# PSUM banks of the state space part: 3, 4 and 1 in place of 2, 5 and 1

## The chip, the cores and the metric

The kernel runs on one core of a Trainium2 chip. The metric is device time in microseconds (us) of one launch. A core has a matrix engine (TensorE, PE in the rows), three engines for elementwise work (VectorE or DVE, ScalarE or ACT, GpSimd or POOL), a queue engine (SyncE, SP) and DMA engines. TensorE writes its results to PSUM, which has eight banks of 128 x 512 floats; the other engines read them there.

## The reference

An encoder trunk of two layers works on x (256 tokens x 1024) and on a memory of 256 tokens. Layer 0 mixes tokens by a bidirectional diagonal state space layer (S5) with a gated output, layer 1 by dilated attention; each layer then attends to the memory and has an MLP of width 4096. What matters here is the state space layer, and the keys and values of the memory:

```
def s5_direction(u, lam_re, lam_im, log_dt, b_re, b_im, c_re, c_im, reverse):
    ...
    bu_re = jnp.einsum('bsgc,gpc->bsgp', u, bbar_re)
    bu_im = jnp.einsum('bsgc,gpc->bsgp', u, bbar_im)
    ...
    _, _, xr, xi = lax.associative_scan(combine, (a_re, a_im, bu_re, bu_im),
                                        reverse=reverse, axis=1)
    return jnp.einsum('bsgp,gcp->bsgc', xr, c_re) - jnp.einsum('bsgp,gcp->bsgc', xi, c_im)

def memory_cross_attention(h, mem_n, w_q, w_kv, w_o, g_q, g_k):
    ...
    kv = (mem_n @ w_kv).reshape(bsz, mlen, 2, MEM_HEADS, MEM_HEAD_DIM)
```

There are 64 groups of 16 channels, 64 states each, and two directions. The keys and values are a product of 256 x 1024 by 1024 x 2048 for each of the two layers.

## The kernel before

The program is written as straight code, and a scheduler decides in what order the instructions stand on each engine and which free PSUM bank a tile gets. Tiles of PSUM come from three pools: `psa()` for accumulators (pool pa), `psb()` for everything of the chunks (pb) and `pss()` (ps). The sizes of the pools are the three numbers of `banks`. A tile that finds no free bank waits for the last reader of the tile that had it.

The state space layer goes over eight chunks of eight groups, numbered 0 to 7. For each chunk there are these steps:

- **Weighing-in** (`s5_weigh_in`): VectorE forms V in six operations (L1053, L1054, L1055, twice), TensorE transposes it into two `psb` tiles (L1060, four transposes each), ScalarE copies them to VT (L1062). V and VT have one buffer each.
- **Drive**: TensorE multiplies VT with the input into two `psb` tiles (L1099, 32 instructions).
- **Scan**: VectorE turns the drive (L1114 to L1119), scans it (L1123, twice) and turns it back (L1126 to L1131), in place in the two banks of the drive; the last two write xt. ScalarE prepares R for the scan (L1109, L1110) and copies xt to its place behind it (L1134, L1135).
- **Impulse**: TensorE multiplies the weights of the chunk (L1162, 16 instructions, one `psb` tile), ScalarE copies the result (L1167), VectorE adds to it (L1169, twice), ScalarE's queue writes it to memory (L1172) and reads it back in another layout as M (L1178, four issues).
- **Read**: TensorE multiplies the scan's states and M (L1191, L1194; 24 instructions, one `psb` tile), ScalarE applies the gelu (L1197, tile G), TensorE transposes G (L1203, another `psb` tile), ScalarE rounds it (L1207) and VectorE takes the rest (L1208).

GpSimd prepares the turns of each scan and the weights of each read meanwhile.

Between the steps of the chunks stand the memory products: three of the four halves of the keys and values (`memory_part` through `gemm32`). They have six blocks of 512 columns; a block has two `psa` tiles and 16 matmul instructions (L248, fp32, 128 x 512), 96 instructions in all. The trace has two records for each fp32 matmul instruction. ScalarE evacuates the tiles (L334). Behind the state space part the banks are split 4 and 4. There the last quarter of the memory product runs (L207 to L209, in three passes of rounded parts, whose weights ScalarE rounds at L161 and VectorE at L162), then the gated output and everything else.

Of the kernel before, what the change touches and what calls it, by code (L numbers as in the profile page):

```python
# [1269 lines left out]
def trunk(tc, a, stages=("s0", "x0", "m0", "d1", "x1", "m1")):  # L1270
    with ExitStack() as ctx:
        k = Trunk(ctx, tc, a)
# [21 lines left out]
        keys = [None, None]  # L1294
        if "s0" in seq:
            kvt = tc.alloc_tile_pool(name="kvt", bufs=1)
            with k.banks(2, 5, 1):
                with tc.tile_pool(name="s5", bufs=1) as ph:
                    with tc.tile_pool(name="s5p", bufs=1) as pr:
                        k.load_gains(pr, early, nc.sync)  # L1300
                        k.s5_load(pr, kv[0][1], kv[1])
                        k.s5_params(pr)
                        mT = [k.memory_in(0, kvt, kv[0][1])]
                        k.s5_norm(ph, kv[0][0].rearrange("p a b -> p (a b)"))
                        k.s5_tables(ph)
                        k.s5_b(ph)
                        turns = k.s5_turns(pr, ph, k.h.rearrange("p t c -> p (t c)"))
                        k.s5_weigh_in(ph, 0)
                        k.s5_c(ph, pr)
                        k.s5_skip(ph, pr)  # L1310
                        k.s5_input(ph)
                        mr = k.row_rstd(kv[0][1], "mem")
                        mT.append(k.memory_in(1, kvt, kv[0][1]))
                    gT = k.new_x()
                    with tc.tile_pool(name="s5m", bufs=1) as mp:
                        k.s5(mp, ph, turns, gT)
                        k.load_gains(mp, late, nc.sync)
                        k.bias_rows()
                xin()
                k1 = right("k1")  # L1320
                k.wq = right("wq")
                k0 = tc.alloc_tile_pool(name="k0", bufs=1, side="right")
                k.memory_part(0, 0, kv[0][0], mT[:1], mr, k.kvw)
                k.memory_part(0, 1, kv[0][1], mT[:1], mr)
                k.memory_part(1, 0, kv[1][0], mT[1:], mr)
        else:
            with k.banks(4, 4), tc.tile_pool(name="kvt", bufs=1) as kvt:
                k.load_gains(kvt, early, nc.sync)
                k.load_gains(kvt, late, nc.sync)
                k.bias_rows()  # L1330
                mem = kvt.tile([P, 2, D], F32, tag="mem", name="mem")
                k.memory_load(mem)
                mr = k.row_rstd(mem, "mem")
                k1 = right("k1")
                k.wq = right("wq")
                k0 = tc.alloc_tile_pool(name="k0", bufs=1, side="right")
                for q in range(2):
                    if "x%d" % q in seq:
                        mT = [k.memory_in(q, kvt, mem)]
                        for i in range(2):  # L1340
                            k.memory_part(q, i, kv[q][i], mT, mr)
                        keys[q] = k.key_parts(q, k.key_norms(q, kv[q][0], kvt), (k0, k1)[q])
                xin()
# [69 lines left out]
```

## Time and profile before

| | us |
|---|---|
| runs | 1066.17, 1064.74, 1066.33 |
| median | 1066.17 |
| profiled execution | 1063.59 |
| its span in the trace | 1061.8 |

The span is the time between the first and the last instruction of the profiled execution; the metric lies 1.8 us above it. The state space part takes about the first 208 us of it. In the rows "PEclk", the number behind the busy times of a window, is the share of TensorE's full clock that was granted.

### The profile page before, as it was taken

What the parts mean: (1) busy time and instruction counts of PE and PEld (TensorE: products, weight loads), DVE (VectorE), ACT (ScalarE), POOL (GpSimd) and SP (SyncE); (2) the same over time, 40 slices, a digit from 0 to 9 for tenths busy, and PEclk for the clock granted to TensorE, in tenths of its full rate; (3) what the DMA queues carried; (4) which work ended last, traced back from release to release, by engine and by line L of the source; (5) the groups of instructions that cost most, each with busy time, mean ns of one, the idle gap of its engine ahead of it and who ended that gap; (6) DMA issues with size and microseconds to landing.
All of it is one profiled execution on the core that took longest, in us unless ns stands there. A gap on an engine that the chain in (4) does not pass through costs nothing.

```text
span 1061.8 us, 17001 instructions
## 1 busy us (share of the span) xinstructions
PE 1012.3 (95%) x6591; PEld 830.8 (78%) x6591; DVE 696.8 (66%) x1108; ACT 576.5 (54%) x1030; POOL 210.7 (20%) x186
## 2 busy tenths in 40 slices
PE   4888889989999999999999999999999999999998
PEld 3454555568898998899878878878788989889996
DVE  7798995456586645544587777778747775544444
ACT  7453553576675644444555656667545655444443
POOL 3998981030000011000040030000200001100000
PEclk8898899999999999999999999999999999999999
DMA  9322233465543455565565555555415244555552
GB/s 199 104 90 70 56 108 112 129 218 182 179 136 109 166 192 191 170 192 192 180 213 165 159 168 178 159 162 149 149 60 173 106 157 162 178 193 185 188 188 100
DMA packets 98429, 163.80 MB, mean 154 GB/s; under 512 B 16704, under 2 KB 27116, under 8 KB 98092
## 3 DMA queue, kind: packets, MB, share of 16 engines
q1 hardware_dynamic: 89052, 158.84, 47.1%
q10 hardware_dynamic: 9296, 3.87, 1.4%
q8 instruction: 52, 0.85, 0.3%
q14 instruction: 29, 0.24, 0.1%
HBM read 160.70 MB, written 3.83 MB: 155 GB/s over the span
## 4 chain that ended last, share of the span: by engine, by line
PE 78%; DVE 12%; ACT 3%; issue 1%; POOL 1%; ACTq 0%; DVEq 0%
PE psa L208 14%; PE psa L209 14%; PE psa L207 14%; PE psb L279 6%; PE psb L283 6%; PE psb L281 6%; PE psa L405 4%; PE psa L248 3%; PE psb L390 2%; DVE wlo L162 2%; DVE V L1055 1%; PE psb L534 1%; DVE psb L1123 1%; ACT whi L161 1%; PE psb L673 1%
## 5 line engine op out<-in xcount | busy, mean ns | idle before, releaser
L162 DVE TENSOR_TENSOR wlo<-raw,whi 128x1024 fp32r<-128x1024 f32 x264 | 333.0, 1262 | 229.1 <-ACT whi L161 226.4
L161 ACT CAST whi<-raw 128x1024 fp32r<-128x1024 f32 x264 | 276.6, 1048 | 224.2 <-PE psa L209 139.2
L207 PE MATMUL psa<-whi,xs 128*128 128x512 f32 x448 | 177.8, 397 | 0.5 <-ACT sg L1238 0.5
L209 PE MATMUL psa<-whi,xs 128*128 128x512 f32 x448 | 176.8, 395 | 0.0
L208 PE MATMUL psa<-wlo,xs 128*128 128x512 f32 x448 | 176.3, 394 | 0.0
L279 PE MATMUL psb<-xs,whi 128*128 128x256 f32 x512 | 145.3, 284 | 0.0
L281 PE MATMUL psb<-xs,whi 128*128 128x256 f32 x512 | 145.3, 284 | 0.0
L283 PE MATMUL psb<-xs,wlo 128*128 128x256 f32 x512 | 145.1, 283 | 0.0
L292 POOL TENSOR_TENSOR sq<-rl 128x512 f32<-128x512 f32 x32 | 40.0, 1252 | 524.0 <-ACT rl L291 524.0
L209 PE MATMUL psa<-whi,hl 128*128 128x512 f32 x256 | 101.6, 397 | 0.0
L208 PE MATMUL psa<-wlo,hh 128*128 128x512 f32 x256 | 101.6, 397 | 0.0
L207 PE MATMUL psa<-whi,hh 128*128 128x512 f32 x256 | 101.5, 396 | 0.0
L248 PE MATMUL psa<-raw,mT 128*128 128x512 f32 x192 | 97.6, 654 | 2.9 <-ACT k L334 2.9
L279 PEld LDWEIGHTS psb<-xs,whi 128*128 128x128 f32 x512 | 98.3, 192 | 0.9 <-DVE xs L184 0.4
L281 PEld LDWEIGHTS psb<-xs,whi 128*128 128x128 f32 x512 | 98.3, 192 | 0.5
L283 PEld LDWEIGHTS psb<-xs,wlo 128*128 128x128 f32 x512 | 98.4, 192 | 0.0
L207 PEld LDWEIGHTS psa<-whi,xs 128*128 128x128 f32 x448 | 84.3, 188 | 16.9 <-ACT sg L1238 0.9
L209 PEld LDWEIGHTS psa<-whi,xs 128*128 128x128 f32 x448 | 84.2, 188 | 16.6
L208 PEld LDWEIGHTS psa<-wlo,xs 128*128 128x128 f32 x448 | 84.3, 188 | 15.9
L248 PEld LDWEIGHTS psa<-raw,mT 128*128 128x128 f32 x192 | 37.5, 207 | 43.2 <-issue 38.1
L209 PEld LDWEIGHTS psa<-whi,hl 128*128 128x128 f32 x256 | 48.3, 189 | 11.5
L207 PEld LDWEIGHTS psa<-whi,hh 128*128 128x128 f32 x256 | 48.3, 189 | 11.0
(330 smaller groups left out, 1542.0 us busy)
## 6 DMA issues: line engine op xcount, KB each, us to landing
raw<-in_mlp_w SPq DMA_DIRECT2D x128, 512.0 KB, 3.7
raw<-in_attn_w_qkv SPq DMA_DIRECT2D x72, 512.0 KB, 3.6
raw<-in_xattn_w_kv SPq DMA_DIRECT2D x32, 512.0 KB, 3.9
raw<-in_s_w_glu SPq DMA_DIRECT2D x16, 512.0 KB, 4.3
raw<-in_xattn_w_q SPq DMA_DIRECT2D x16, 512.0 KB, 3.4
raw<-in_xattn_w_o SPq DMA_DIRECT2D x16, 512.0 KB, 3.5
raw<-in_attn_w_o SPq DMA_DIRECT2D x8, 512.0 KB, 3.9
bias_d<-bias_o SPq DMA_DIRECT2D x1, 1536.0 KB, 8.8
```

The costliest lines, as they stand in the source:

```text
L161: self.nc.scalar.copy(hi, src)
L162: self.nc.vector.tensor_sub(lo, src, hi.bitcast(F32))
L207: nc.tensor.matmul(acc[t], xh[:, k0 + k, sl], hi[:, k % 2, :], start=st, stop=False)
L208: nc.tensor.matmul(acc[t], xh[:, k0 + k, sl], lo[:, k % 2, :], start=False, stop=False)
L209: nc.tensor.matmul(acc[t], xl[:, k0 + k, sl], hi[:, k % 2, :], start=False, stop=en)
L248: nc.tensor.matmul(acc[t], xT[:, k + q, t * P:(t + 1) * P], raw[:, q, :], start=k + q == 0, stop=k + q == KT - 1)
L279: nc.tensor.matmul(o, hi[:, k % 2, fs], xh[:, kt, :], start=st, stop=False, skip_group_check=True)
L281: nc.tensor.matmul(o, hi[:, k % 2, fs], xl[:, kt, :], start=False, stop=False, skip_group_check=True)
L283: nc.tensor.matmul(o, lo[:, k % 2, fs], xh[:, kt, :], start=False, stop=en, skip_group_check=True)
L292: nc.gpsimd.tensor_mul(sq, rl, rl)
L390: self.nc.tensor.matmul(out, x[p], w[q], start=start and i == 0, stop=stop and i == 2)
L405: nc.tensor.matmul(o, p[:, kt, ts], q[:, k, :], start=kt == 0 and t == 0 and i == 0, stop=kt == 7 and t == 1 and i == 2, skip_group_check= ...
```

## The change

The two numbers say how many banks the accumulators of the memory products get and how many the tiles of the chunks get. Two and five become three and four; the third pool keeps its one bank.

```
         if "s0" in seq:
             kvt = tc.alloc_tile_pool(name="kvt", bufs=1)
-            with k.banks(2, 5, 1):
+            with k.banks(3, 4, 1):
                 with tc.tile_pool(name="s5", bufs=1) as ph:
```

Everything else follows from the scheduler, which places the instructions anew. On TensorE, this is the difference between drive 0 and drive 2, early in the loop over the chunks. L1099 is a drive, L1162 an impulse, L1060 the transposes of a weighing-in, L248 a memory product.

```order
 L1099 MATMUL psb<-u_503,VT 64x64 x32
-L248 MATMUL psa<-raw,mT 128x512 x3
 L1060 MATMUL psb<-ident,V 128x128 x8
 L248 MATMUL psa<-raw,mT 128x512
 L1099 MATMUL psb<-u_503,VT 64x64 x32
+L248 MATMUL psa<-raw,mT 128x512 x6
 L1162 MATMUL psb<-wk,bb 32x112 x16
-L248 MATMUL psa<-raw,mT 128x512 x10
+L248 MATMUL psa<-raw,mT 128x512 x5
 L1060 MATMUL psb<-ident,V 128x128 x8
-L248 MATMUL psa<-raw,mT 128x512 x3
+L248 MATMUL psa<-raw,mT 128x512 x8
```

Products move behind drive 1: from three, one, ten and three, 17 in all, to one, six, five and eight, 20 in all. Further on in the loop about ten products stand between two drives in the change, and the eight transposes of a weighing-in are split four and four with products between. Counted over the program, 73 of the 96 products stand ahead of drive 7 before, and 86 in the change; 23 and 10 follow it.

On TensorE at the end of the state space part, from the products ahead of read 7 on (L1203 there is the transpose of chunk 6), the kernel before has these rows:

```order
L248 MATMUL psa<-raw,mT 128x512
L1203 MATMUL psb<-ident,G 64x64 x8
L248 MATMUL psa<-raw,mT 128x512 x11
L1191 MATMUL psb<-W,xs 64x64 x4
L1194 MATMUL psb<-M,u_503 64x64 x2
```

The changed kernel has these at the same place:

```order
L248 MATMUL psa<-raw,mT 128x512
L1203 MATMUL psb<-ident,G 64x64 x8
L248 MATMUL psa<-raw,mT 128x512
L1191 MATMUL psb<-W,xs 64x64 x4
L1194 MATMUL psb<-M,u_503 64x64 x2
```

Eleven products ahead of read 7 have become one. Of the four products that stand between read 7 and the first L207 before, none is left in the change.

On VectorE at the end of scan 7, L1208 of chunk 6 moves from between the operations of the scan to behind them, as this piece of the difference shows (the L162 of mp belongs to what follows the state space part).

```order
 L1126 TENSOR_TENSOR tmp<-psb,xs 128x512
 L1127 TENSOR_TENSOR tmp<-psb,xs 128x512
-L1208 TENSOR_TENSOR xs<-psb,xs 128x256
 L1128 TENSOR_TENSOR psb<-psb,xs 128x512
 L1129 TENSOR_TENSOR psb<-psb,xs 128x512
 L1130 TENSOR_TENSOR xt<-tmp,psb 128x512
 L1131 TENSOR_TENSOR xt<-tmp,psb 128x512
+L1208 TENSOR_TENSOR xs<-psb,xs 128x256
```

The scan's last operations no longer stand behind L1208. In the same way L1208 of chunk 0 moves from the start of scan 2 to behind it, and L1169 of chunk 0 from scan 0 to behind it, into the weighing-in that follows. Behind the state space part, 16 transposes of the keys (L379) move on TensorE behind the first products of the gated output.

## Rows read from the trace of the kernel before

**Rows 1.** The page: the span, and busy time of each engine.

```profile
span 1061.8 us, 17001 instructions
...
PE 1012.3 (95%) x6591; PEld 830.8 (78%) x6591; DVE 696.8 (66%) x1108; ACT 576.5 (54%) x1030; POOL 210.7 (20%) x186
```

**Rows 2.** Windows: length; busy PE, PEld, DVE, ACT, POOL (instructions); PEclk; DMA share; GB/s.

```profile
60.00:171.00 111.00, 94.51 (x1090) 56.16 (x1091) 103.39 (x153) 50.39 (x95) 92.90 (x78) 0.88 0.29 88
171.00:208.66 37.66, 36.71 (x345) 19.18 (x343) 15.90 (x24) 16.72 (x29) 0.00 (x0) 1.00 0.36 107
208.66:1061.00 852.34, 838.26 (x4866) 728.05 (x4866) 530.65 (x809) 472.47 (x832) 76.62 (x56) 1.00 0.52 167
```

**Rows 3.** VectorE's timeline in the loop: start, us, engine, line, operation, [idle <-releaser].

```profile
60.07 0.69 DVE L1114 TENSOR_TENSOR tmp<-psb,xs 128x512 f32<-128x512 f32 x1
...
69.19 0.23 DVE L1169 SCALAR_TENSOR_TENSOR kx<-eye,dc,psb 128x16 f32<-128x16 f32 x1 [1.80 <-ACT kx L1167]
...
97.31 0.42 DVE L1208 TENSOR_TENSOR xs<-psb,xs 128x256 fp32r<-128x256 f32 x1 [3.52 <-ACT xs L1207]
...
144.02 0.69 DVE L1114 TENSOR_TENSOR tmp<-psb,xs 128x512 f32<-128x512 f32 x1
...
154.18 0.68 DVE L1053 TENSOR_TENSOR tmp<-pss,bb 128x512 f32<-128x512 f32 x1
...
160.34 0.69 DVE L1114 TENSOR_TENSOR tmp<-psb,xs 128x512 f32<-128x512 f32 x1
```

**Rows 4.** TensorE's timeline in the loop: a product's wait, drive 5.

```profile
64.07 1.18 PE L248 MATMUL psa<-raw,mT 128*128 128x512 f32 x2 [2.93 <-ACT k L334]
...
138.94 1.16 PE L1099 MATMUL psb<-u,VT 64*64 64x64 f32 x64
```

**Rows 5.** Windows of L248 alone: length; busy PE, PEld (records); PEclk; DMA share; GB/s.

```profile
24.00:60.00 36.00, 21.97 (x36) 7.92 (x36) 0.86 0.36 90
60.00:171.00 111.00, 52.05 (x106) 20.64 (x107) 0.88 0.29 88
171.00:208.66 37.66, 23.59 (x52) 8.95 (x50) 1.00 0.36 107
```

**Rows 6.** TensorE's timeline in the tail, up to the first L207.

```profile
189.59 9.71 PE L248 MATMUL psa<-raw,mT 128*128 128x512 f32 x22
199.23 0.45 PE L1191 MATMUL psb<-W,xs 128*64 128x64 f32 x8
...
201.81 1.13 PE L248 MATMUL psa<-raw,mT 128*128 128x512 f32 x2
...
204.49 2.84 PE L248 MATMUL psa<-raw,mT 128*128 128x512 f32 x6
...
208.66 0.50 PE L207 MATMUL psa<-whi,mp 128*128 128x512 f32 x1 [0.95 <-ACT k L334]
```

**Rows 7.** TensorE's timeline at read 0.

```profile
87.00 0.70 PE L1191 MATMUL psb<-W,xs 128*64 128x64 f32 x8 [3.64 <-DVE xt L1130]
...
91.14 5.10 PE L248 MATMUL psa<-raw,mT 128*128 128x512 f32 x6
```

**Rows 8.** Window at read 0, columns as in rows 2.

```profile
88.00:92.00 4.00, 4.00 (x40) 2.89 (x38) 3.83 (x8) 3.91 (x7) 3.84 (x4) 0.50 0.00 0
```

**Rows 9.** VectorE's timeline at scan 7.

```profile
174.42 0.69 DVE L1114 TENSOR_TENSOR tmp<-psb,xs 128x512 f32<-128x512 f32 x1 [3.55 <-issue]
...
190.11 0.42 DVE L1208 TENSOR_TENSOR xs<-psb,xs 128x256 fp32r<-128x256 f32 x1 [0.60 <-ACT xs L1207]
...
192.25 0.68 DVE L1131 TENSOR_TENSOR xt<-tmp,psb 128x512 f32<-128x512 f32 x1
```

**Rows 10.** ScalarE's timeline in the tail (ACTq: its DMA issues).

```profile
190.17 2.53 ACTq L1178 DMA_DIRECT2D M<-kd  x4
192.96 1.04 ACT L1134 COPY xs<-xt 64x1024 f32<-64x1024 f32 x1 [2.88 <-DVE xt L1131]
...
201.98 0.38 ACT L1197 ACTIVATE G<-psb 128x256 f32<-128x256 f32 x1 [6.92 <-PE psb L1194]
```

More of the change, by code (lines that the diff above doesn't have):

```diff
@@ L1296, in trunk @@
             kvt = tc.alloc_tile_pool(name="kvt", bufs=1)
-            with k.banks(2, 5, 1):
+            with k.banks(3, 4, 1):
                 with tc.tile_pool(name="s5", bufs=1) as ph:
```

## The prediction

> **What bounds the kernel now.** I read the page first: a span of 1061.8 us, and TensorE busy for 1012.3 us of it [rows 1]. That average of 95% hides stages, so I cut the span into windows next [rows 2]. From 208.66 us on, TensorE works 838.26 of 852.34 us at a granted clock of 1.00; nothing in PSUM's split can shorten that. Between 60 and 171 us it is VectorE that is full (103.39 of 111 us) while TensorE has 94.51 us of work and a mean clock of 0.88. Between 171 and 208.66 us TensorE is full again (36.71 of 37.66) and VectorE is not (15.90). So the state space part is a loop on VectorE, which leaves TensorE room, and a tail on TensorE, which does what didn't fit. Work that moves from the tail into the loop is a gain as long as VectorE doesn't feel it.
>
> VectorE's timeline shows the loop's beat [rows 3]: scan 0 begins at 60.07, scan 6 at 160.34. Between two scans lies the weighing-in of a later chunk, six operations, 154.18 to 160.34, so 6.2 us. In the timeline there are two stalls: 1.80 us at L1169, which waits for the copy of the impulse response, and 3.52 us at L1208, which waits for L1207. TensorE's timeline shows what the memory products wait for a bank: once, 2.93 us [rows 4]. And by the windows of L248 the 192 records of the products (two for each of the 96 instructions) take 21.97 + 52.05 + 23.59 = 97.61 us [rows 5]; 0.883 us each would be 84.8 us (9.71 us for 22 records, 11 products [rows 6]). The other 12.8 us is the half clock: TensorE waited 3.64 us for scan 1, and from there on three products take 5.10 us, 1.70 us each [rows 7]; in 88 to 92 us the granted clock is 0.50, the lower level, 1.2 GHz [rows 8].
>
> **What the change does, and its cost.**
>
> *Thirteen products move forward.* By the order, 73 products stand ahead of drive 7 before, 86 in the change; 23 and 10 follow it. The third bank lets a product of the next block be issued before the last block is evacuated. In the tail 13 x 0.883 = 11.5 us of TensorE's work goes; in the loop it comes.
>
> *Is there room in the loop?* The loop's TensorE work would be 94.51 + 11.5 = 106.0 us, in 111 us less the two stalls, 105.7. That is full on paper, but 12.8 us of it is the half clock, paid wholly before 171 us (at 171 to 208.66 the clock is 1.00, and 52 records at 0.44 us are 23.0 of the 23.59). With TensorE fuller its wait of 3.64 us, behind which the clock fell, becomes shorter. Work other than products is 94.51 - 52.05 = 42.5 us there, 6.1 us for each of seven chunks; with ten products at full clock, 8.8 us, a chunk is 14.9 us. VectorE's beat at the end of the loop is 160.34 - 144.02 = 16.3 us [rows 3]. It fits, with 1.4 us to spare.
>
> *One bank less for the chunks.* Each drive needs two of four banks and now takes those of the scan before; the order shows that from drive 3 on it waits for the scan's last operation (L1131). In before that happens already at drives 5 to 7: drive 5 begins at 138.94 and VectorE goes into scan 5 at 144.02 without a stall [rows 3, 4], since the weighing-in of 6.2 us lies between; the drive takes 1.16 us. So the drive may come up to 6.2 - 1.16 = 5.0 us late at no price. I cost the bank at 0 in the loop. Without that cover each late microsecond is paid in each of the last five chunks. Behind a late drive on TensorE stand the impulse and read of the same chunk, and for these VectorE waits at L1169 and L1208.
>
> *The two stalls.* L1169 of chunk 0 goes behind the scan, into the weighing-in, and L1208 of chunk 0 behind scan 2: what they waited for is then done. So -1.80 and -3.52, -5.3 us for the loop. Bounds: 0 (L1208 of a later chunk stalls in its place) and -5.3; I take -5.3, since scan 5, with an L1169 and an L1208 inside it as the later scans of the change have them, takes 10.2 us from 144.02 to 154.18 and the timeline shows no wait in it [rows 3].
>
> *The tail.* Scan 7 starts behind a wait of 3.55 us for drive 7 [rows 9]. In the change half of the chunk's transposes wait for scan 6 to give a bank back; behind them stand three products (2.65 us) and the drive itself (1.16 us), in sum 3.8 us and a little: about the same, so nothing is gained there. Up to the scan proper the order is unchanged. L1208 of chunk 6 then leaves VectorE's row in scan 7: -0.60 for its wait and -0.42 for itself, -1.0 us [rows 9]. The last scan, which ended at 192.93, ends at 192.93 - 5.3 - 1.0 = 186.6 us.
>
> *Read of chunk 7.* In before it begins at 199.23, 6.30 us after the scan, for 11 products stand ahead of it (189.59 + 9.71 us [rows 6]). In the change one product does, so it waits for the two copies of 1.04 us on ScalarE. These stand behind four DMA issues, 2.53 us from 190.17 [rows 10], which move with the loop alone: 184.9 to 187.4. Then 2.1 us of copies: read at 189.5, against 199.23: -9.7 us.
>
> *What that empty TensorE costs.* Its last product now ends about 4 us before read 7. [rows 7] has the same figure: after a wait of 3.64 us, read 0 ran from 87.00 to 91.14, 4.14 us, at the lower clock; read 7 in before took 199.23 to 201.81, 2.58 us [rows 6]. So +1.6 us (bounds 0 and 1.6). Behind read 7 comes a hand-over on ScalarE: G at 201.98, then casts, to the first L207 at 208.66, 6.7 us [rows 6, 10]. Before, products (1.13 + 2.84 us) lay in it, so that the wait ahead of L207 was 0.95 us; now none do. The hand-over itself stays (its casts and copies are the same, except two L334 that were done earlier; I take 0 for these, they were partly hidden). But L207 would start at the lower clock. Bounds: 0, and a cold stretch as long as that of [rows 7], 87.00 to 96.17, 9.2 us for work of 2.58 + 2.65 us at full clock, so 4.0 us. I take the middle, 2.0.
>
> **Sum.** -9.7 + 1.6 + 2.0 = -6.1 us. Behind 208.66 us only 16 transposes of keys move; 0. The profiled execution took 1063.59 us, 1.8 us more than its span; it becomes 1057.5. The median of the runs is 1066.17, and 1066.17 - 6.1 = 1060.1 us. About 0.2%, 2.1 us, is what a measurement can tell here.
>
> **The rivals.**
>
> *Nothing comes of it (about 1066).* For it: the products waited only once for a bank, 2.93 us, so the third bank removes no wait worth the name; what moves is work, and if TensorE stays at the lower clock for the same 12.8 us in the loop, then 106.0 us doesn't fit there, the late drives eat the 5.3 us of stalls, and what read 7 gains over that (9.7 - 5.3 = 4.4 us) goes to the two cold starts (at their bounds 1.6 + 4.0 = 5.6). Sum: between -1.2 and +1.2. Against it: drive 5 is chained to the scan in before too, and ran in 1.16 us there [rows 4].
> The Trainium skill has a rule that speaks for this rival: its page "TensorE: Matmul & The Clock Gate", section "A second HAM failure mode: psum-queue depth-cycling", tells of a kernel that went round its PSUM banks and lost clock between bursts, so that throughput fell although a single product was as fast as elsewhere. By that rule going round three banks beside four would keep the lower clock in the loop, and the time would be this rival's. The trace agrees in so far as the clock falls in the loop, but it does so behind the wait for scan 1 [rows 7], and with two banks; no row here shows it to depend on their number.
>
> *Slower (about 1070).* The mechanism: the four banks chain each drive to the scan before, and the chunk to the drive. If a drive comes later than those 5.0 us, VectorE stalls, the scan ends later, the bank comes later, TensorE waits longer and goes to half clock: ten products then take 17.0 instead of 8.8 us, and a chunk costs 14.9 + 8.2 = 23.1 us and, with the rest of its work slow too, up to 25, where VectorE's beat is 16.3. From a stall of 6.1 / 5 = 1.2 us in each of the five chained chunks on, the gain is gone; one chunk at half clock, some 9 us, brings 1069 to 1070. Against it: the products in the loop are what keeps TensorE busy, and there are more of them.
>
> *More (about 1056.5).* No cold start, -9.7 us. For it: no row shows the clock behind an empty stretch at this place, and before it TensorE will have worked without a break. Against it: [rows 7] shows it fall behind a stretch of the same size.
>
> **How the numbers follow.** My forecast's family (a gain of 3 to 9.7 us, the last rival in it with 0.15) has 0.69, nothing 0.17, slower 0.14. The forecast's own range is 1056 to 1063. For 8 in 10 the range reaches into the middle rival on the upper side: from 1055 (the last rival, less the 1.4 us by which the runs of before differ among themselves) to 1067.
>
> **What would show it.** Right: scan 6 starts about 155 us instead of 160.34, no VectorE stall over 1 us between scans 0 and 6; no product between L1203 of chunk 6 and read 7 but one; read 7 at 189 to 190; L207 at about 200; the clock below 1 there for some microseconds. Wrong: stalls at L1114 (the drive late) or L1208 in chunks 3 to 6, a clock of 0.5 in the loop longer than before, a hand-over longer than 6.7 us, or a stretch behind it that takes longer than 852 us by more than 4.

## The result

The changed kernel takes 1056.46 us (four runs, 1055.19 to 1057.14); the kernel before took 1065.45 us in the four runs beside them (1064.40 to 1066.33). The ratio is 0.9918, with a 95% interval of 0.9906 to 0.9930, so 9.0 us less, between 7.5 and 10. Run again on the chip of the last experiments it gave 1056.37 against 1064.84 us, 0.9925 [0.9909, 0.9941]. The forecast was 1060.1 us in a range of 1055 to 1067.

The profiled execution of the changed kernel took 1056.39 us. Its page begins like this (compare [rows 1]):

```profile
span 1054.6 us, 17000 instructions
...
PE 1008.3 (96%) x6591; PEld 829.1 (79%) x6591; DVE 693.5 (66%) x1108; ACT 577.0 (55%) x1030; POOL 210.2 (20%) x186
```

TensorE's busy time fell by 4.0 us, the span by 7.2. These are the windows of the loop (scan 0 to scan 6), of the tail up to the first L207, and of the rest; columns as in [rows 2]:

```profile
62.58:153.62 91.04, 86.74 (x1036) 49.44 (x1036) 88.95 (x135) 48.95 (x94) 87.90 (x75) 1.00 0.32 96
153.62:199.84 46.22, 37.30 (x404) 20.38 (x402) 26.40 (x43) 20.68 (x37) 6.72 (x6) 0.90 0.35 109
199.84:1053.80 853.96, 840.66 (x4866) 730.58 (x4866) 530.78 (x810) 471.96 (x831) 76.62 (x56) 1.00 0.51 166
```

The loop of the kernel before, cut in the same way at its scans, was this:

```profile
60.07:160.34 100.27, 86.27 (x1024) 51.12 (x1024) 92.90 (x134) 47.12 (x87) 89.66 (x76) 0.88 0.30 90
```

The loop is 9.2 us shorter, and its granted clock is 1.00 where it was 0.88; TensorE does 86.74 us of work in it, where it did 86.27 in 9 us more before; it stands empty for 4.3 us of the loop, before for 14.0. The tail has a clock of 0.90 now, and TensorE stands empty for 9 us of it.

VectorE's timeline gives the points to hold against [rows 3] and [rows 9]:

```profile
62.58 0.69 DVE L1114 TENSOR_TENSOR tmp<-psb,xs 128x512 f32<-128x512 f32 x1 [0.66 <-PE psb L1099]
...
153.62 0.69 DVE L1114 TENSOR_TENSOR tmp<-psb,xs 128x512 f32<-128x512 f32 x1
...
165.32 0.37 DVE L1169 SCALAR_TENSOR_TENSOR kx<-eye,dc,psb 128x16 f32<-128x16 f32 x2 [1.27 <-ACT kx L1167]
167.93 0.69 DVE L1114 TENSOR_TENSOR tmp<-psb,xs 128x512 f32<-128x512 f32 x1 [2.23 <-issue]
...
184.84 0.68 DVE L1131 TENSOR_TENSOR xt<-tmp,psb 128x512 f32<-128x512 f32 x1
```

And TensorE's timeline the end of the tail, which answers to [rows 6]:

```profile
183.90 1.13 PE L248 MATMUL psa<-raw,mT 128*128 128x512 f32 x2
188.84 0.45 PE L1191 MATMUL psb<-W,xs 128*64 128x64 f32 x8 [3.81 <-issue]
...
197.98 0.69 PE L489 MATMUL psb<-junk,tb 33*24 33x160 f32 x2 [1.72 <-DMA junk<-in_bias_onehot]
199.84 0.79 PE L207 MATMUL psa<-whi,mp 128*128 128x512 f32 x1 [1.17 <-ACT junk L490]
```

The ledger of the two profiled executions, stretch by stretch:

| stretch | before | after | difference | forecast |
|---|---|---|---|---|
| up to scan 0 | 60.07 | 62.58 | +2.5 | 0 |
| scan 0 to scan 6 | 100.27 | 91.04 | -9.2 | -5.3 |
| scan 6 to the end of scan 7 | 32.59 | 31.90 | -0.7 | -1.0 |
| end of scan 7 to read 7 | 6.30 | 3.32 | -3.0 | -3.4 |
| read 7 to L207 | 9.43 | 11.00 | +1.6 | +1.6 |
| L207 to the end | 853.1 | 854.8 | +1.6 | +2.0 |
| sum | 1061.8 | 1054.6 | -7.2 | -6.1 |

Four of the six terms are where they were forecast, to within 0.4 us. The loop gave 3.9 us more, and the start took 2.5 us; neither was forecast. Between scans 6 and 7 VectorE waits 1.27 us for an impulse and 2.23 us for drive 7, 3.5 us as before.

**Read 7 and the hand-over.** One product (183.90) stands between L1203 of chunk 6 and read 7, which begins at 188.84 after a wait of 3.81 us. The hand-over has a wait for a transfer (1.72 us, the table of the bias) and one for ScalarE (1.17 us). What came of that wait, and of the hand-over, is in the clock of two windows of the changed kernel:

```profile
189.00:193.00 4.00, 3.48 (x48) 2.58 (x46) 0.00 (x0) 0.56 (x2) 0.00 (x0) 0.65 0.00 0
199.84:203.84 4.00, 4.00 (x9) 3.13 (x10) 1.57 (x3) 3.14 (x16) 0.00 (x0) 0.50 0.68 236
```

Read 7 ran at a mean clock of 0.65, and the products from L207 on began at 0.50, the lower of the two levels: nine of them fit into four microseconds, where 17 began in the first four of the kernel before. These are the two cold starts of the forecast: read 7 took some 1.4 us longer than before (3.9 instead of 2.6 us), and the first nine products 1.8 us longer (4.00 instead of 2.20).

**The loop's other 3.9 us.** Between scans 0 and 6 no wait is left on VectorE's timeline; in before there were 1.80 and 3.52 us. The rest is in a line that the forecast took as constant. This is VectorE's timeline of the kernel before in the weighing-in ahead of scan 4:

```profile
123.27 1.58 DVE L1055 TENSOR_TENSOR V<-tmp 128x512 f32<-128x512 f32 x1
...
126.20 1.47 DVE L1055 TENSOR_TENSOR V<-tmp 128x512 f32<-128x512 f32 x1
```

and this GpSimd's, at the same time (POOL; start, us, line):

```profile
123.23 1.06 POOL L774 TENSOR_TENSOR pt<-h 128x512 f32<-128x512 f32 x1
124.37 1.60 POOL L775 TENSOR_TENSOR xs<-pt 128x512 f32<-128x512 f32 x1
126.06 1.07 POOL L772 TENSOR_TENSOR pt<-h 128x512 f32<-128x512 f32 x1
```

The same line in the changed kernel, in the weighing-in ahead of scan 4:

```profile
118.14 0.69 DVE L1055 TENSOR_TENSOR V<-tmp 128x512 f32<-128x512 f32 x1
```

with GpSimd at that time:

```profile
116.95 1.28 POOL L1147 TENSOR_TENSOR W<-pt 128x512 f32<-128x512 f32 x1
118.31 1.48 POOL L1145 TENSOR_TENSOR pt<-taq,ct 128x512 f32<-128x512 f32 x1
```

L1055, whose two inputs both lie in SBUF, takes 0.69 us when it begins as one of GpSimd's operations ends (118.14; L1147 ended at 118.23), and then it is GpSimd's next operation that is long (1.48 us, where L1145 takes 1.10 elsewhere). When it begins inside one of GpSimd's operations (123.27, in L774 from 123.23 on; 126.20, in L772 from 126.06 on), it takes 1.58 and 1.47 us; the first ends 0.56 us after L774, and the L775 behind it is long in its turn (1.60 us). So, by these rows, whichever comes first goes on and the other waits. The Trainium skill says the same on its page "SBUF — State Buffer", section "SBUF: two separate sides": VectorE and GpSimd share a pair of ports, which is locked for a whole instruction, against VectorE's instructions with two inputs in SBUF among others. The trace agrees, with up to 1.0 us for one L1055 (1.70 us at the longest). Over the loop, windows of L1055 alone show the 12 operations of the kernel before, and then of the changed one (columns: length; busy VectorE; granted clock; DMA share; GB/s):

```profile
60.07:160.34 100.27, 17.34 (x12) 0.88 0.30 90
```

```profile
62.58:153.62 91.04, 13.47 (x12) 1.00 0.32 96
```

That is 17.34 against 13.47 us, 3.9 us. With the two stalls, 5.3 us, this is the loop's 9.2 us. The change has touched neither engine's work here: it moved the moment at which a weighing-in falls among GpSimd's operations. The new moment comes again in every profile: in the seven later ones of kernels with this order in the loop (e4, e6 and e8 to e12, below) the loop takes 91.03 to 91.08 us and L1055 13.5 us of it.

### The profile page after: what moved, and what is told of

The parts are those of the page before. It is cut to its first block, busy times and chain, and to the rows that moved or that the text cites. A ratio compares the mean times of both kernels' runs of the same rounds, so it can differ in the third digit from the quotient of the medians.

```text
span 1054.6 us, 17000 instructions
## 1 busy us (share of the span) xinstructions
PE 1008.3 (96%) x6591; PEld 829.1 (79%) x6591; DVE 693.5 (66%) x1108; ACT 577.0 (55%) x1030; POOL 210.2 (20%) x186
## 4 chain that ended last, share of the span: by engine, by line
PE 81%; DVE 12%; ACT 4%; issue 2%; DMA 1%; POOL 0%; SPq 0%; ACTq 0%; DVEq 0%
PE psa L209 15%; PE psa L208 15%; PE psa L207 15%; PE psb L279 6%; PE psb L283 6%; PE psb L281 6%; PE psa L248 4%; PE psa L405 4%; PE psb L390 2%; DVE wlo L162 2%; ACT whi L161 1%; PE psb L534 1%; DVE psb L1123 1%; DVE V L1055 1%; PE psb L673 1%
## 5 line engine op out<-in xcount | busy, mean ns | idle before, releaser
L162 DVE TENSOR_TENSOR wlo<-raw,whi 128x1024 fp32r<-128x1024 f32 x264 | 331.5, 1257 | 228.9 <-ACT whi L161 225.3
L207 PE MATMUL psa<-whi,xs 128*128 128x512 f32 x448 | 177.6, 396 | 0.7 <-ACT sg L1238 0.7
L207 PE MATMUL psa<-whi,hh 128*128 128x512 f32 x256 | 101.4, 396 | 0.0
L207 PEld LDWEIGHTS psa<-whi,xs 128*128 128x128 f32 x448 | 84.2, 188 | 17.1 <-ACT sg L1238 1.2
L208 PEld LDWEIGHTS psa<-wlo,xs 128*128 128x128 f32 x448 | 84.3, 188 | 15.9
L248 PE MATMUL psa<-raw,mT 128*128 128x512 f32 x192 | 94.3, 630 | 0.0
L248 PEld LDWEIGHTS psa<-raw,mT 128*128 128x128 f32 x192 | 36.0, 201 | 35.7 <-issue 34.5
L208 PEld LDWEIGHTS psa<-wlo,hh 128*128 128x128 f32 x256 | 48.3, 189 | 11.1
```

Of the source, the lines that this page charges most:

```text
L162: self.nc.vector.tensor_sub(lo, src, hi.bitcast(F32))
L207: nc.tensor.matmul(acc[t], xh[:, k0 + k, sl], hi[:, k % 2, :], start=st, stop=False)
L208: nc.tensor.matmul(acc[t], xh[:, k0 + k, sl], lo[:, k % 2, :], start=False, stop=False)
L248: nc.tensor.matmul(acc[t], xT[:, k + q, t * P:(t + 1) * P], raw[:, q, :], start=k + q == 0, stop=k + q == KT - 1)
```

## The experiments

Before the first of them I held two theories against each other. **Mine**: the third accumulator bank moves products into the loop, which helps read 7; two stalls go; L1055 meets GpSimd less often; the empty TensorE costs two cold starts. **The rivals**: the four banks of the chunks alone do it; or the rest of the 9 us has another origin (the start, the clock). Beside every experiment the kernel before ran on the same chip.

**e1: two accumulator banks, four for the chunks.**

```
-            with k.banks(2, 5, 1):
+            with k.banks(2, 4, 1):
```

> Two accumulator banks, four for the chunks, one bank unused. By the order the chunks take the form of the changed kernel (transposes split four and four, drives behind the scan), but 23 products stay behind drive 7 and 11 ahead of read 7, as before. My account (the third accumulator bank moves the products, and that is what read 7 gains): no gain at read 7, which stays some 6.3 us behind scan 7; the loop may lose the 1.80 us stall at L1169 but keeps one at L1208 of chunk 0, which stays inside scan 2; 1062 to 1067 us. Rival (the four banks of the chunks alone order the loop better, the third accumulator bank is worth nothing): 1056 to 1058 us, as the changed kernel.

Measured: 1058.68 us against 1064.15, ratio 0.9943 [0.9923, 0.9963], between the two expectations. VectorE's timeline shows where it stands with the stall and the last scan (columns as before):

```profile
96.19 0.42 DVE L1208 TENSOR_TENSOR xs<-psb,xs 128x256 fp32r<-128x256 f32 x1 [3.51 <-ACT xs L1207]
...
169.21 0.69 DVE L1114 TENSOR_TENSOR tmp<-psb,xs 128x512 f32<-128x512 f32 x1 [1.22 <-PE psb L1099]
...
184.93 0.68 DVE L1131 TENSOR_TENSOR xt<-tmp,psb 128x512 f32<-128x512 f32 x1
```

and TensorE's what stands ahead of read 7, and L207:

```profile
183.78 9.71 PE L248 MATMUL psa<-raw,mT 128*128 128x512 f32 x22
193.42 0.45 PE L1191 MATMUL psb<-W,xs 128*64 128x64 f32 x8
...
202.85 0.50 PE L207 MATMUL psa<-whi,mp 128*128 128x512 f32 x1 [0.95 <-ACT k L334]
```

The stall at L1208 of chunk 0 is there (3.51 us), that at L1169 is gone, and read 7 is 7.8 us behind the end of scan 7 (184.93 + 0.68) because 11 products stand ahead of it (3.3 in the changed kernel): so much of my account holds, that the third accumulator bank is what read 7 gains from. But the last scan ends at 185.61 instead of 192.93, 7.3 us earlier, without any third accumulator bank. The loop is 3.1 us shorter (97.17 us; 1.8 of it the stall, and L1055 takes 15.90 us in it, 1.4 less), scan 6 to scan 7 is 2.1 us shorter (scan 7 waits 1.22 instead of 3.55 us for drive 7), and scan 7 itself is 2.1 us shorter. From scan 6 to the end of scan 7 it takes 28.41 us, the changed kernel 31.90, with its waits of 1.27 and 2.23 us: the third accumulator bank loses 3.5 us there, and which part of the new order does it is not isolated. So by the medians the bank taken from the chunks gives 5.5 us by itself (3.9 to 8.2 by the interval), and the third accumulator bank 3.0 to 3.5 us on top (9.0 and 8.5 less 5.5). By the profiles, from scan 0 to L207, the two give 5.8 and 5.6 us (148.59 us before, 142.82 in e1, 137.26 in the changed kernel). e1 and the changed kernel never ran on one chip, and their intervals overlap, so how the 9 us divide between the two banks is known to a few microseconds only. The forecast had booked the loss of a bank at 0.

**e2 and e3: GpSimd's work in the loop left out, before and after the change.** The turns of chunks 2 to 7 and the weights of reads 1 to 7 aren't formed:

```
         def turn(ch):
+            if ch > 1:
+                return
...
         def weigh_out(ch):
+            if ch > 0:
+                Ws[ch] = Ws[0]
+                return
...
```

> The kernel before with GpSimd's turns of chunks 2 to 7 and weights of reads 1 to 7 left out: those of chunks 0 and 1 are used again, so the output isn't the reference's. The order on TensorE stays. If L1055 is long because GpSimd works at the same time, each L1055 takes 0.7 us, the six weighings-in of the loop 4.3 us each instead of 4.8 to 6.0, and the loop gets some 7 us shorter, less what the products then lack of time in it: 1058 to 1062 us. If its length has another reason, the weighings-in stay at 33.7 us in sum and the time within 2 us of 1065.5.

> The changed kernel with the same work of GpSimd left out. With L1055 at 0.7 us its weighings-in fall from 29.9 to about 26 us, so by some 4 us: 1052 to 1054 us. The distance to the kernel before with the same left out then shows the change without the part that came from GpSimd's timing: 5 to 6.5 us, where it was 9.0. If that timing had no part in it, the distance stays at 9.

Measured: 1056.66 us and 1053.80 us, against 1064.15 (0.9919 [0.9897, 0.9942] and 0.9905 [0.9887, 0.9923]). e3 is where it was expected, e2 below its 1058 to 1062 us. L1055 in the loop, first e2 and then e3:

```profile
60.12:153.09 92.97, 8.29 (x12) 0.89 0.30 88
```

```profile
64.78:150.72 85.94, 8.29 (x12) 1.00 0.37 107
```

Twelve operations take 8.29 us in both, 0.69 us each: GpSimd was what made them long. The loops are 92.97 and 85.94 us. Put together from the unchanged kernels they should be 100.27 - 17.34 + 8.29 = 91.2 and 91.04 - 13.47 + 8.29 = 85.9 us; the second fits to 0.1 us, the first is 1.8 longer. The waits of e2's loop say why (its lines lie six further down from there on, so L1175 is L1169 and L1214 is L1208):

```profile
69.26 0.23 DVE L1175 SCALAR_TENSOR_TENSOR kx<-eye,dc,psb 128x16 f32<-128x16 f32 x1 [1.81 <-ACT kx L1173]
...
94.83 0.42 DVE L1214 TENSOR_TENSOR xs<-psb,xs 128x256 fp32r<-128x256 f32 x1 [3.33 <-ACT xs L1213]
...
110.21 0.43 DVE L1214 TENSOR_TENSOR xs<-psb,xs 128x256 fp32r<-128x256 f32 x1 [0.38 <-ACT xs L1213]
...
128.21 0.42 DVE L1214 TENSOR_TENSOR xs<-psb,xs 128x256 fp32r<-128x256 f32 x1 [1.61 <-ACT xs L1213]
```

The two known stalls are there (1.81 and 3.33 us), and L1208 now waits in two more chunks, 0.38 and 1.61 us, since VectorE got faster and TensorE didn't. The four waits add up to 7.1 us and the two loops differ by 7.0. So once GpSimd's timing is taken out, the change's gain in the loop is the waits for TensorE. And 7.0 of the loop's 9.2 us stay without that timing: only 2.2 us of the gain hang on it, not the whole 3.9, for a VectorE that isn't held up by GpSimd waits longer for TensorE in the order of before. Between the medians only 2.9 us are left, where 5 to 6.5 were expected. The profiles give a reason, though for the other executions it isn't shown: e3 began scan 0 at 64.78 us and e2 at 60.12, and from scan 0 on e3 is 9.3 us shorter (986.8 against 996.1 us).

**e4 and e12, e9, e10, e11: TensorE kept busy in the tail.** Six matmuls of no use go ahead of read 7 and six between the two L489; e9 has only the first, e10 only the second, e11 is the changed kernel itself, e12 is e4 once more.

```
             ps = self.psb()
+            if ch == 7:
+                for _ in range(6):
+                    nc.tensor.matmul(ps[:, 256:512], self.ident,
+                                     self.xt7[:, 0].rearrange("p g k -> p (g k)")[:, :256],
+                                     start=True, stop=True, skip_group_check=True)
             for i in range(4):
...
+            if gs[0]:
+                for _ in range(6):
+                    nc.tensor.matmul(ps[:, 256:512], self.ident,
+                                     self.xt7[:, 0].rearrange("p g k -> p (g k)")[:, :256],
+                                     start=True, stop=True, skip_group_check=True)
             nc.tensor.matmul(ps[:24, :c1 - c0], tb, e[:33, :c1 - c0], start=True, stop=True)
```

> The changed kernel with six added matmuls on data of no use ahead of read 7 (they wait for the last scan, 0.44 us each) and six more between the two L489 of the hand-over, so that TensorE does not stand empty there. If the empty TensorE is what put read 7 and the first L207 at the lower clock, read 7 takes 2.6 instead of 3.9 us and the first nine products behind L207 0.23 instead of 0.43 us each: 2 to 3 us less, 1053.5 to 1054.5 us. Rival (the clock falls there whatever TensorE does, or the added work takes as long as it gives): 1056 to 1058 us.

e4 gave 1049.12 us (four runs, 1048.82 to 1049.25) against 1064.15, 0.9860 [0.9846, 0.9874]: 7 us below the changed kernel, where 2 to 3 were expected. Its scan 0 began at 58.93 where the changed kernel's began at 62.58, in the same order of instructions. The next four runs, on one chip, tell whether that belongs to the kernel, and what each half of the added matmuls gives:

> The changed kernel with the six added matmuls ahead of read 7 alone. Read 7 at the full clock (2.6 instead of 3.9 us), the hand-over as in the changed kernel: 1.3 us less than e11. If e4's early start was a property of that kernel's executions, tied to neither of the two stretches, scan 0 starts at 62.6 us here again; if it came with the matmuls of the tail, at 58.9.

> The changed kernel with the six added matmuls in the hand-over alone. Read 7 stays at the lower clock, the products behind L207 get up to 2.0 us back: 0.5 to 2 us less than e11. For the start as for e9.

> The changed kernel itself, on the chip of these runs, as the measure for the other three: 1055 to 1058 us, 8 to 10 us below the kernel before.

> The kernel of e4 once more. If the clock at its start is a property of the kernel, the runs lie at 1049 us with a clock of 0.996 again. If it was luck, most of them lie at 1052 to 1054 us with a clock of about 0.985 to 0.99, 2.5 to 4 us below e11: the tail's part alone.

| | median, us | range | ratio to before (1064.84) |
|---|---|---|---|
| e11, changed kernel | 1056.37 | 1054.26 to 1059.07 | 0.9925 [0.9909, 0.9941] |
| e9, ahead of read 7 | 1053.49 | 1051.79 to 1056.52 | 0.9899 [0.9882, 0.9916] |
| e10, in the hand-over | 1054.79 | 1052.41 to 1055.05 | 0.9902 [0.9886, 0.9918] |
| e12, both | 1052.59 | 1051.38 to 1053.84 | 0.9888 [0.9872, 0.9904] |

e12 is 3.8 us below e11, in the upper part of the 2.5 to 4 expected. The intervals of e9 and e10 overlap with that of e11, so for the halves the profiles are the better guide. In e9 read 7 ran at the full clock, and from read 7 to L207 it took 9.87 us instead of 11.47 (e11):

```profile
185.00:189.00 4.00, 2.79 (x50) 2.17 (x52) 0.00 (x0) 1.39 (x4) 0.00 (x0) 1.00 0.02 4
```

and in e10 the first products behind L207 (nine in the same four microseconds of the changed kernel, 15 here):

```profile
200.97:204.97 4.00, 3.65 (x15) 2.67 (x16) 3.29 (x3) 3.74 (x11) 0.00 (x0) 1.00 0.85 253
```

But the matmuls of the hand-over have a price. Their 12 records are these, in e4 and in e12:

```profile
190.60 2.86 PE L491 MATMUL psb<-xt,ident 128*128 128x256 f32 x12
```

```profile
193.88 4.72 PE L491 MATMUL psb<-xt,ident 128*128 128x256 f32 x12
```

In e12 they ran mostly at the lower clock themselves, in e10 too (4.26 us), and read 7 to L207 took 12.51 us in e12 and 13.38 in e10, longer than e11's 11.47; in e4 it took 9.60. What e10 and e12 gain lies behind L207: 852.0 and 852.1 us, against 857.7 in e11 and 854.8 in the first profile of the changed kernel. There the order on TensorE has changed with the added matmuls (two L207 come first, and one wait of 1.84 us stands where e11 has 0.64 and 2.29), so that these runs don't tell the clock's part from the order's.

The early start of e4 doesn't belong to the kernel either. The windows of e4 and of e12, the same kernel, over the same stretch of the start:

```profile
18.00:24.00 6.00, 5.24 (x48) 5.24 (x48) 5.90 (x27) 6.00 (x12) 1.31 (x2) 1.00 1.10 265
```

```profile
18.00:24.00 6.00, 5.29 (x48) 5.29 (x48) 5.90 (x27) 6.00 (x11) 1.41 (x2) 0.50 1.08 250
```

The clock is 1.00 in one and 0.50 in the other, and scan 0 (L1119 here, with five lines added above) begins at 58.93 and 61.14 us, first e4 and then e12:

```profile
58.93 0.69 DVE L1119 TENSOR_TENSOR tmp<-psb,xs 128x512 f32<-128x512 f32 x1 [0.66 <-PE psb L1104]
```

```profile
61.14 0.69 DVE L1119 TENSOR_TENSOR tmp<-psb,xs 128x512 f32<-128x512 f32 x1 [0.66 <-PE psb L1104]
```

The two profiles differ by 4.7 us: e4 gains 2.2 at the start and 2.9 from read 7 to L207, both times at the higher clock, and loses 0.4 behind it. Of the changed kernel itself, scan 0 began at 62.58 in the first profile and at 58.35 in e11's; in 44 to 48 us the granted clock was 0.50 in the first and 1.00 in the second. So the +2.5 us of the ledger is less than the start of one kernel varies by, and isn't shown to be a cost of the change. Why all four executions of e4 lay within 0.5 us of one another, at a mean clock of 0.996, isn't known; they were on another chip than e12.

**e5, e6 and e8: matmuls at the start.** To take that variation out, four matmuls of no use went into the empty stretch of TensorE before 18 us, in the kernel before (e5), the changed one (e6) and e4 (e8).

```
         ps = self.pss()
+        for _ in range(4):
+            nc.tensor.matmul(ps, self.ident, self.kv01[:, 0, :512], start=True, stop=True, skip_group_check=True)
         for q, x in enumerate(rows(av)):
...
```

> The kernel before with four added matmuls of 128 x 512 on data of no use (0.88 us each at the full clock) in the empty stretch of TensorE between 13 and 18 us, so that the clock doesn't fall there. If the scatter between executions, and part of the 9.0 us, comes from whether the clock of the start falls, the granted clock before 30 us becomes 1.00, all runs lie within 1 us of one another, and scan 0 starts up to 2 us earlier: 1060 to 1063 us. If the start has nothing to do with it, 1063 to 1066 us with the same scatter.

> The changed kernel with the same four matmuls. If the late start of scan 0 (62.58 us against 60.07) is the clock's, it starts at 58 to 60 us and the time is 1051 to 1054 us, with the distance to the kernel before with the same matmuls at 8 to 10 us. If it is the order's (products between the transposes of the input), scan 0 still starts 2 us later than in the kernel before with the same matmuls, and the distance is 6 to 7 us.

> The changed kernel with the four matmuls at the start and the twelve of e4 in the tail. If e4's gain was 3.6 us of start clock and the rest in the tail, this gives what e4 gave: 1048 to 1050 us. If e4's start was luck of its executions, this is better than e6 by the tail alone, 2 to 3 us.

Measured: 1065.49 (1.0012 [1.0001, 1.0023]), 1059.33 (0.9953 [0.9939, 0.9968]) and 1057.14 us (0.9931 [0.9911, 0.9951]), against 1064.44; 1060 to 1063 and 1051 to 1054 us were expected of e5 and e6. The aim was missed: the added work changed the order, and in e6 TensorE waits 6.45 us for a copy on ScalarE ahead of the first weighing-in's transposes (L1063, L1060 in the others), where it waited 2.62 us for VectorE in the changed kernel:

```profile
35.07 1.94 PE L1063 MATMUL psb<-ident,V 128*128 128x128 f32 x8 [6.45 <-ACT k L999]
```

The clock falls in the start all the same (0.67 in 24 to 30 us of e6), and all three begin scan 0 late, at 64.6 to 65.2 us. One thing they do tell. Scan 0 begins at 64.66 us in e5 and at 64.62 in e6, so here the start is equal, and the distance is 6.2 us by the medians and 8.2 by the profiles; their loops are 98.10 and 91.08 us. e5's is 2.2 us shorter than that of the kernel before, mostly because the stall at L1169 (1.80 us) is absent in it: that stall hung on the start, too, and not on the banks alone. e8 gained 2.2 us on e6 by the matmuls in the tail.

**e7: three banks for the chunks.**

```
-            with k.banks(2, 5, 1):
+            with k.banks(3, 3, 1):
```

> Three accumulator banks and three for the chunks, one bank unused: by the order 90 products stand ahead of drive 7 and six behind it, against 86 and ten in the changed kernel. My account: a drive keeps two of the three banks, so the transposes, impulse, read and L1203 go one by one through the third, VectorE waits 1 us or more in most chunks at L1114, L1169 or L1208, and what the fewer products give is lost: 1056 to 1064 us. Rival (the fewer banks the chunks have, the better the order): 1050 to 1054 us.

Measured: 1065.30 us over 12 runs from 1057.99 to 1074.23, ratio 1.0015 [0.9992, 1.0039] without the longest: no better than before, and above the 1056 to 1064 us expected. The profiled execution was the longest of them, 9 us above the median. VectorE's waits in it are, among others:

```profile
82.23 0.37 DVE L1169 SCALAR_TENSOR_TENSOR kx<-eye,dc,psb 128x16 f32<-128x16 f32 x2 [4.03 <-ACT kx L1167]
...
145.02 1.18 DVE L1055 TENSOR_TENSOR V<-tmp 128x512 f32<-128x512 f32 x1 [3.08 <-PE psb L1060]
...
181.46 0.42 DVE L1208 TENSOR_TENSOR xs<-psb,xs 128x256 fp32r<-128x256 f32 x1 [6.60 <-ACT xs L1207]
```

VectorE waits for the impulse (4.03 us), inside a weighing-in for the transposes that hold V (3.08) and for L1207 (6.60). That these waits make the other executions slow as well is not shown. From five banks to four was a gain of 5.5 us for the chunks; from four to three, at three accumulators, is a loss of some 9 (1065.30 against 1056.4 us, on different chips).

## Why the prediction held, and where it was off

**The direction held, and the mechanism in part.** Thirteen products left the tail, the loop had room for them, read 7 began 3.3 us behind the last scan (2.9 forecast, 6.3 before), the two stalls went, and both cold starts came. The sum was 6.1 us, the measured gain 9.0 by the first runs and 8.5 by e11. But a good part of the gain, 5.5 us by e1, comes without the third accumulator bank and without the products that it moves, from the step that the forecast had put at 0.

**Is there room in the loop?** Yes, but not by the sum of the forecast. Of the 12.8 us of half clock only 5.3 lay in the loop (52.05 us for 106 records [rows 5], where 0.883 for two would be 46.8); 6.1 lay ahead of 60 us (21.97 for 36 records, 15.9 at that price) and could make no room in it. In the changed kernel those are still there (21.18 us for 34 records from 24 us to scan 0). Windows of L248 alone, from scan 0 to scan 6, before and after (columns as in [rows 5]):

```profile
60.07:160.34 100.27, 47.70 (x96) 18.50 (x96) 0.88 0.30 90
```

```profile
62.58:153.62 91.04, 54.59 (x120) 21.60 (x120) 1.00 0.32 96
```

Twelve products more took 6.9 us more, since of the 5.3 us all but 1.6 came back. That was enough. What the forecast said of TensorE's wait held: the 3.64 us ahead of read 0 are gone. The longest waits of TensorE in the loop, of the kernel before and of the changed one, are these:

```profile
121.42 1.74 PE L1162 MATMUL psb<-wk,bb 128*32 128x112 f32 x32 [4.48 <-DVE xt L1130]
```

```profile
140.13 0.69 PE L1203 MATMUL psb<-ident,G 128*64 128x64 f32 x16 [1.53 <-ACT G L1197]
```

e1, without the third accumulator bank, still has a wait of 3.35 us (at 84.37), with a clock of 0.73 in 88 to 100 us. In the list of what would show it, the clock was the right place.

**One bank less for the chunks, at 0.** This step was mis-sized. The cover of 5.0 us did hold (no wait at L1114 between scans 1 and 6), but the step asked only what the lost bank costs. e1 shows that it brings 5.5 us by itself: with four banks the scheduler put the steps of the chunks into an order in which VectorE waits less.

**The loop, -5.3.** The stalls were right to 0.1 us. The term lacked the 3.9 us of L1055, because the weighing-in was taken as 6.2 us whatever GpSimd does. The trace of before had the sign: L1055 takes 0.82 us at 88.76 and 1.59 us at 155.56, in the same step of two chunks. That 3.9 us is luck as far as the forecast goes: a timing of this order that came out well, every time, and that nothing in the number of banks asks for. e2 and e3 show that 7.0 us of the loop's 9.2 don't need it.

**Behind 208.66, 0 for the key transposes.** Not quite. In before they lay in TensorE's waits there; now these waits lie together. The changed kernel's timeline of TensorE, 20 us behind the first L207:

```profile
219.45 0.50 PE L207 MATMUL psa<-whi,mp 128*128 128x512 f32 x1 [0.63 <-ACT whi L161]
222.24 0.50 PE L208 MATMUL psa<-wlo,mp 128*128 128x512 f32 x1 [2.29 <-DVE wlo L162]
```

The same place in e11:

```profile
215.96 0.49 PE L207 MATMUL psa<-whi,mp 128*128 128x512 f32 x1 [0.64 <-ACT whi L161]
218.74 0.79 PE L208 MATMUL psa<-wlo,mp 128*128 128x512 f32 x1 [2.29 <-DVE wlo L162]
```

and e11's window right behind it:

```profile
218.00:224.00 6.00, 5.26 (x12) 4.13 (x13) 4.65 (x3) 0.16 (x1) 2.44 (x1) 0.50 0.50 143
```

The waits are the same (0.63 and 2.29 us), but in e11 the clock fell behind them, to 0.50, and the gated output's first L207 came 30.7 us behind the first L207 of all, where the first profile has 27.9. In e9 it fell too, in e6 not. The term is about 0 or 2.8 us, by the execution.

**The rivals.** "Nothing comes of it" needed the lower clock to stay in the loop; it left. (Its 12.8 us had the same error as above, and the lower end of its sum, -1.2, doesn't follow from its terms: 1.6 + 2.0 less 4.4 is -0.8.) The rule of the Trainium skill that spoke for it, of the page "TensorE: Matmul & The Clock Gate", section "A second HAM failure mode: psum-queue depth-cycling", is not borne out here: three banks beside four went round at a clock of 1.00, where two beside four had 0.92 (e1) and two beside five 0.88. "Slower" needed drives more than 5 us late; none was in the changed kernel, and the longest execution of e7 shows what it can look like when the chunks do run short. "More" named 1056.5 us, the time that was measured, by luck: both of the cold starts that it did without were there, and what made up for them it didn't have.

**What stays open.** Why the clock falls at the start in most of the profiled executions and not in some, with the same instructions, the runs don't tell; nor why all of e4's executions were quick. How the 9 us divide between the bank taken away and the bank added is known to a few microseconds only. How the 5.5 us of e1 divide between the order and L1055's timing in it is only bounded (1.4 us for L1055).

## What to carry to other kernels

PSUM banks decide, through the scheduler, which work may be early, so a new split is a new order: read the order for what stands ahead of the instruction that the tail waits for, and measure each pool's change alone (here the bank taken away gave no less than the bank added). Where a tail loses its filler, ask what keeps TensorE busy there; added work of no use gave 3.8 us (e12 against e11) and 2.2 (e8 against e6), so real work moved there may give as much; that wasn't run. And before a difference of 2 us between two traces is explained, look at the clock of the start in a second profile of the same kernel.

## What was not expected of the hardware

- VectorE's L1055 takes 0.69 us alone and up to 1.70 us beside GpSimd, and GpSimd's L1145 1.10 alone and 1.48 behind an L1055: 9.1 us of the loop of the kernel before (17.34 less 8.29), 5.2 us in the changed one.
- The same kernel starts scan 0 at 58.35 or 62.58 us, with a granted clock of 1.00 or 0.50 in 44 to 48 us; single executions of one kernel spread over as much as 8.1 us (e1: 1052.28 to 1060.41), nearly the 9.0 of the change.
- Behind waits of 0.63 and 2.29 us the granted clock fell in two executions (e9, e11) and not in two others (the first profile, e6), with the same instructions there.
